# SBUF rooms of a hybrid decoder layer: the place of every take read from a table, in columns cut anew

## The chip, the cores and the metric

The kernel runs on one core of one Trainium2 chip, in one launch. The metric is the device time of one execution in microseconds. Before the change it is 1494.37 us, the median of three runs that lie between 1493.93 and 1495.05 us.

On the core, TensorE (PE in the profile; its weight loads are PEld) does the matrix products into PSUM. VectorE (DVE), ScalarE (ACT) and GpSimd (POOL) do the element-wise work. SyncE (SP) issues the DMAs; its queue is SPq in the rows.

## The reference, cut to what matters

One step of one decoder layer over 512 prompt tokens, 16 meta tokens and 32 sampled tokens (8 sequences of 4), 560 columns in all. The model is 1024 wide, the feed-forward 2816.

```python
h = x + 0.5 * rms_norm(swiglu(rms_norm(x, ffn1_pre_g), ffn1_w_gate, ffn1_w_up, ffn1_w_down), ffn1_post_g)
u = rms_norm(h, mix_pre_g)
proj = u @ w_in
q_a, k_a, v_a, gk_low, r_a, q_b, k_b, v_b, gate_a, gate_b = jnp.split(proj, offs, axis=-1)
...
o_a, s_new = gla_branch(q_a, k_a, v_a, g, s0.astype(f32), lead)
o_b = sb_attend(q_b, keys, vals, sb_bias, q_off).reshape(B, L, SB_W)
m = jax.nn.sigmoid(gate_a) * (o_a @ w_o_gla) + jax.nn.sigmoid(gate_b) * (o_b @ w_o_sb)
h = h + rms_norm(m @ w_out, mix_post_g)
y = h + 0.5 * rms_norm(swiglu(rms_norm(h, ffn2_pre_g), ffn2_w_gate, ffn2_w_up, ffn2_w_down), ffn2_post_g)
```

All values are float32. `gla_branch` is a gated linear recurrence in chunks of 64 tokens, four heads; `sb_attend` is stick-breaking attention, sixteen heads, over a paged cache for the sampled tokens.

## The kernel before, in words

**Products.** Activations lie with the feature on the partition and the 560 tokens along the row, in two halves of 280 columns. Each float32 factor is split in two fp32r parts, `hi` and `lo`, and each product is three matmuls: hi·hi, hi·lo, lo·hi (L686, L687, L689; L699, L700, L702; L1253 to L1255 and others). A weight block takes this road: SP loads it to a buffer `raw` (a pool of three; issued at L186 or L625), ACT casts it to `hi` (L665, L964), DVE subtracts to get `lo` (L153, the shared helper `tt`), and PE uses it. Many feed-forward tiles use a seven-product scheme on quarters of the blocks (`seven`, L1253 to L1255), the others the plain eight (`eight`).

**Stages.** FFN1, then the mixer (projections, the GLA heads, the stick-breaking heads, gates and output projections), then FFN2. Each feed-forward ends with its down projection (class `Down` and `k_steps`).

**What sets the order.** The program is written as one stream of steps. `step()` is called between groups of matmuls; `later(n, f)` puts a piece of element-wise work n steps ahead. For PE, DVE, ACT and POOL the order so written is kept (`manual_schedule`, L1462). The order of SP is not in that list: there the scheduler places each DMA where its buffer is ready, so the order in which SP issues loads and stores depends on when a buffer's last user is done.

**Rooms.** Everything that isn't in a fixed tile or a ring of the pools lives in an `Arena`: 150 units of 280 float32 columns, cut into columns: before, 20 long columns of 6 units and 15 short ones of 2. `take(width, dt)` hands out a run of free units in one column, a "room"; `give` returns it. A column holds one type (F32 or F32R) at a time. When an empty column changes its type it gets a new tile under the same tag, in the same bytes, and the first write to that tile waits for all that used the old one. A write to a room of a tile that goes on waits for whoever read or wrote those bytes last. So the place of a room decides for whom its first writer waits, and on SP also where a load stands. Before the change, `take` tries every free run and picks the one with the least key: it keeps four long columns in reserve, avoids runs at odd units, avoids rooms given less than `RECENT` = 14 steps ago, and among the rest takes the one that has been free longest.

**Names used below.** `h_again` (L1297 to L1299) loads the eight blocks of the FFN1 input `h` back from DRAM into rooms while the down projection of FFN1 runs. `fetch_early` (L635 to L638) loads a 512 KB weight block of the mixer's v projection to a room, ahead of its time. L1600 loads the 16 columns of `w_in` that give the low-rank gate, 64 bytes to a piece, into a room `wg16`; the DVE operation at L1602 multiplies them by `g_mix`. At L376 POOL clears a quarter of `t3`, a room of a GLA head, which `sample_keys` (L501 to L504) reads first. L469, L495 and L497 are POOL's causal masks of the GLA heads. `hidden` (L931) splits a finished feed-forward tile into rooms for `hi` and `lo`.

Of the kernel before, what the change touches and what calls it, by code (L numbers as in the profile page):

```python
# [9 lines left out]
F32 = mybir.dt.float32  # L10
F32R = mybir.dt.float32r
# [5 lines left out]
P = 128  # L17
# [5 lines left out]
NT = NP + NS + NM  # L23
# [22 lines left out]
MIXER += [("R", "p", 4), ("R", "p", 5), ("S", "b", 6), ("R", "p", 6), ("R", "p", 7)]  # L46
AHEAD = 150
LEAVE = 12
UNITS, LONGS = 150, 20


class Arena:

    UNIT = HW
    LONG, SHORT = 6, 2
    RECENT, RESERVE = 14, 4

    def __init__(self, pool, n, longs):
        self.pool, self.now, self.made = pool, 0, 0
        self.freed = [[-99] * self.LONG for _ in range(longs)]  # L60
        self.freed += [[-99] * self.SHORT for _ in range((n - longs * self.LONG) // self.SHORT)]
        self.tile = [None] * len(self.freed)
        self.held = {}

    def take(self, width, dt=F32, tight=False):
        k = -(-width // self.UNIT)
        best = None
        spare = sum(None not in f for f in self.freed if len(f) == self.LONG)
        for c, free in enumerate(self.freed):
            empty, long = None not in free, len(free) == self.LONG  # L70
            if not empty and self.tile[c].dtype != dt:
                continue
            for s in range(len(free) - k + 1):
                f = free[s : s + k]
                if None in f:
                    continue
                other = empty and self.tile[c] is not None and self.tile[c].dtype != dt
                since = max(free) if other else max(f)
                waste = k % 2 == 0 and s % 2
                alone = k == 1 and free[s ^ 1] is not None  # L80
                opens = empty and long and k <= self.SHORT
                key = (opens and spare <= self.RESERVE, waste, self.now - since < self.RECENT, opens, alone, since)
                if best is None or key < best[0]:
                    best = (key, c, s)
        assert best is not None, f"no room for {width}: {[sum(x is not None for x in f) for f in self.freed]}"
        _, c, s = best
        if None not in self.freed[c] and (self.tile[c] is None or self.tile[c].dtype != dt):
            self.made += 1
            self.tile[c] = self.pool.tile([P, len(self.freed[c]) * self.UNIT], dt, tag=f"room{c}", name=f"room{c}_{self.made}")
        self.freed[c][s : s + k] = [None] * k  # L90
        a = self.tile[c][:, s * self.UNIT : s * self.UNIT + width]
        self.held[id(a)] = (a, c, s, k)
        return a

    def halves(self, a):

        _, c, s, k = self.held.pop(id(a))
        r = a[:, :HW], a[:, HW:]
        for i, t in enumerate(r):
            self.held[id(t)] = (t, c, s + i, 1)  # L100
        return r

    def give(self, *aps):
        for a in aps:
            _, c, s, k = self.held.pop(id(a))
            self.now += 0.001
            self.freed[c][s : s + k] = [self.now] * k


class Parts:  # L110
# [11 lines left out]
def hybrid_step(  # L122
# [29 lines left out]
    def tt(out, a, b, op, eng=None):  # L152
        (eng or V).tensor_tensor(out=out, in0=a, in1=b, op=op)  # L153
# [128 lines left out]
    class Gates:  # L282
# [48 lines left out]
    class Head:  # L331
# [361 lines left out]
    def k_steps(acc, parts, k0, k1, kt, act, halves, nw=P, wid=(HW, HW)):  # L693
        hi, lo = parts
        for k in range(k0, k1):
            a = {h: act.get(k, h, wid[h]) for h in halves}
            wh, wl = hi[k - k0], lo[k - k0]
            for h in halves:
                T.matmul(acc[h][:nw, : wid[h]], wh, a[h][0], start=(k == 0), stop=False)  # L699
                T.matmul(acc[h][:nw, : wid[h]], wh, a[h][1], start=False, stop=False)  # L700
            for h in halves:
                T.matmul(acc[h][:nw, : wid[h]], wl, a[h][0], start=False, stop=(k == kt - 1))  # L702
            step()
# [19 lines left out]
    def later(n, f):  # L723
        todo.append([n, f])
# [314 lines left out]
    def early_tiles(u, rs, wid, nw, hid, pairs, wait, prepare, first=False):  # L1039
# [41 lines left out]
    def other_tiles(old, gain, rs, nw, wid, hid, pairs, plan, late, sums_at, begun):  # L1081
# [373 lines left out]
    for kind, what, n in MIXER:  # L1455
        w, c = {"r": (win, C_RA), "a": (win, C_GA), "b": (win, C_GB), "o": (w_o_gla[0], 0), "p": (w_o_sb[0], 0)}[what]
# [5 lines left out]
    with tc.manual_schedule(engines={E.PE, E.DVE, E.Activation, E.Pool}):  # L1462
# [72 lines left out]
        for j in range(2):  # L1535
            c = slice(P * j, P * j + P)
# [53 lines left out]
        hid = Parts()  # L1590
# [150 lines left out]
        for j in range(5):  # L1741
            n = P if j < 4 else NTL
# [89 lines left out]
    own_, other = (slice(0, 64), slice(64, P)), (slice(64, P), slice(0, 64))  # L1832
# [18 lines left out]
    class Pair:  # L1851
# [181 lines left out]
        at = property(lambda self: self.__dict__.setdefault("at_", {}))  # L2033
# [387 lines left out]
    with tc.manual_schedule(engines={E.PE, E.DVE, E.Activation, E.Pool}):  # L2421
# [5 lines left out]
        starts, n = {}, -24  # L2427
# [40 lines left out]
        for pr in range(9):  # L2468
            now = last = None
            at = {}  # L2470
# [67 lines left out]
            n = 0  # L2538
# [29 lines left out]
        n = 8 * len(PAGES)  # L2568
# [43 lines left out]
        n = 0  # L2612
# [42 lines left out]
        hid, pairs = Parts(), {}  # L2655
# [83 lines left out]
```

## Time and profile before

| | |
|---|---|
| time, median of three | 1494.37 us (1493.93 to 1495.05) |
| the profiled execution's own time | 1495.05 us |
| its span in the profile | 1493.4 us |
| mean granted clock of TensorE | 0.999 |
| instructions in the span | 29839 |
| HBM read / written | 155.06 MB / 24.97 MB |

The span runs from the first to the last instruction; 1.7 us of the execution's time lie around it. Rows of the profile give: line of the kernel, engine, operation, what is written and read (names without buffer numbers), shape, count, and then busy time or duration. An engine's idle time is put down to what ended it (`<-`). In a timeline, a row that stands for several instructions gives the stretch from the first's start to the last's end, and a bracket gives the idle time before it and its end.

### The profile page before, as it was taken

Reading aid. Unit: us, or ns where it says so; the run is one execution under the profiler, and the core shown is the slowest. Engines: PE = TensorE matmul, PEld = TensorE weight load, DVE = VectorE, ACT = ScalarE, POOL = GpSimd, SP = SyncE. Lnnn points to the kernel's source line nnn. Section 1 sums busy time; section 2 is a strip of 40 time slices with the busy share of each in tenths; the row PEclk is TensorE's granted clock in tenths of the full one; section 3 lists DMA queues with packets and bytes.
Section 4 is the critical chain, followed back from the end, with each engine's and each line's share of the span. In section 5 each row is a group of like instructions: output and inputs, shape, how many; then the busy total and the mean of one; then the engine's idle time right before and its main releaser. Section 6 shows DMA issues by size and latency. Waiting matters only on the chain.

```text
span 1493.4 us, 29839 instructions
## 1 busy us (share of the span) xinstructions
PE 1484.9 (99%) x11893; PEld 1434.2 (96%) x11893; DVE 1105.0 (74%) x1961; ACT 778.9 (52%) x1445; POOL 68.3 (5%) x146
## 2 busy tenths in 40 slices
PE   9999999999999999999999999999999999999998
PEld 8999999999999889999898999999999999999998
DVE  5888888855677866877887845777567898888544
ACT  7455454533555656556555543634565555455333
POOL 2000000000000011112111000000000000000000
PEclk9999999999999999999999999999999999999999
DMA  8133333224664584344456766434531333333262
GB/s 252 47 96 100 100 94 104 86 79 123 177 154 124 162 144 100 89 111 116 119 121 181 216 160 184 122 98 137 169 102 63 100 100 99 100 105 93 80 179 88
DMA packets 277229, 181.98 MB, mean 122 GB/s; under 512 B 10428, under 2 KB 255362, under 8 KB 277090
## 3 DMA queue, kind: packets, MB, share of 16 engines
q1 hardware_dynamic: 276786, 180.00, 44.5%
q8 instruction: 94, 1.54, 0.4%
q14 instruction: 45, 0.37, 0.1%
q0 software_dynamic: 288, 0.07, 0.0%
q10 hardware_dynamic: 16, 0.00, 0.0%
HBM read 155.06 MB, written 24.97 MB: 121 GB/s over the span
## 4 chain that ended last, share of the span: by engine, by line
PE 95%; DVE 3%; ACT 1%; issue 1%; DVEq 0%; ACTq 0%
PE acc L1253 8%; PE acc L1254 8%; PE acc L1255 8%; PE acc L686 7%; PE acc L687 7%; PE acc L689 7%; PE acc L699 6%; PE acc L702 6%; PE acc L700 6%; PE acc L1033 2%; PE acc L1034 2%; PE acc L1035 2%; PE acc L1196 1%; PE acc L1193 1%; DVE room L153 1%; PE acc L1194 1%
## 5 line engine op out<-in xcount | busy, mean ns | idle before, releaser
L153 DVE TENSOR_TENSOR lo<-raw,hi 128x1024 fp32r<-128x1024 f32 (+1 forms) x207 | 248.0, 1199 | 106.3 <-ACT hi L665 70.5
L153 DVE TENSOR_TENSOR room<-room,room 128x544 fp32r<-128x544 f32 (+16 forms) x424 | 263.3, 643 | 71.3 <-ACT room L766 16.6
L1253 PE MATMUL acc<-room,hi 128*128 128x280 f32 (+1 forms) x896 | 259.5, 290 | 0.0
L1254 PE MATMUL acc<-room,hi 128*128 128x280 f32 (+1 forms) x896 | 259.1, 289 | 0.0
L1255 PE MATMUL acc<-room,lo 128*128 128x280 f32 (+1 forms) x896 | 258.9, 289 | 0.0
L686 PE MATMUL acc<-room,hi 128*128 128x280 f32 x832 | 244.4, 310 | 0.2 <-DVE room L156 0.2
L687 PE MATMUL acc<-room,hi 128*128 128x280 f32 x832 | 225.2, 289 | 0.0
L964 ACT CAST hi<-raw 128x1024 fp32r<-128x1024 f32 x100 | 104.8, 1052 | 144.7 <-PE acc L1254 70.6
L689 PE MATMUL acc<-room,lo 128*128 128x280 f32 x832 | 172.9, 289 | 0.0
L1254 PEld LDWEIGHTS acc<-room,hi 128*128 128x128 f32 x896 | 168.6, 188 | 0.0
L1255 PEld LDWEIGHTS acc<-room,lo 128*128 128x128 f32 x896 | 168.6, 188 | 0.0
L1253 PEld LDWEIGHTS acc<-room,hi 128*128 128x128 f32 x896 | 168.6, 188 | 0.0
L686 PEld LDWEIGHTS acc<-room,hi 128*128 128x128 f32 x832 | 156.7, 188 | 12.0 <-issue 10.0
L687 PEld LDWEIGHTS acc<-room,hi 128*128 128x128 f32 x832 | 157.1, 189 | 2.8 <-issue 1.9
L665 ACT CAST hi<-raw 128x1024 fp32r<-128x1024 f32 (+1 forms) x107 | 108.2, 1012 | 73.8 <-issue 23.9
L689 PEld LDWEIGHTS acc<-room,lo 128*128 128x128 f32 x832 | 130.2, 188 | 0.0
L964 ACT CAST hi<-room 128x1024 fp32r<-128x1024 f32 x92 | 76.9, 836 | 87.8 <-PE acc L1254 59.4
L153 DVE TENSOR_TENSOR lo<-room,hi 128x1024 fp32r<-128x1024 f32 x92 | 87.8, 955 | 43.4 <-ACT hi L964 43.0
L699 PE MATMUL acc<-room,hi 128*128 128x280 f32 (+2 forms) x388 | 110.8, 295 | 0.0
L153 DVE TENSOR_TENSOR room<-room,acc 128x272 f32<-128x272 f32 (+1 forms) x180 | 76.3, 436 | 45.6 <-PE acc L1035 22.8
L700 PE MATMUL acc<-room,hi 128*128 128x280 f32 (+2 forms) x388 | 108.8, 290 | 0.0
L699 PE MATMUL acc<-room,room 128*128 128x280 f32 (+3 forms) x368 | 108.4, 295 | 0.0
(402 smaller groups left out, 3453.8 us busy)
## 6 DMA issues: line engine op xcount, KB each, us to landing
raw<-in_w_in_dram SPq DMA_DIRECT2D x43, 512.0 KB, 7.3
raw<-in_ffn_w_gate_dram SPq DMA_DIRECT2D x64, 256.0 KB, 3.0
raw<-in_ffn_w_up_dram SPq DMA_DIRECT2D x64, 256.0 KB, 3.4
raw<-in_ffn_w_down_dram SPq DMA_DIRECT2D x36, 448.0 KB, 4.0
raw<-in_w_in_dram SPq DMA_DIRECT2D x40, 256.0 KB, 5.3
out_dram<-room SPq DMA_DIRECT2D x36, 256.0 KB, 3.4
room<-in_cache_k_dram SPq DMA_DIRECT2D x32, 256.0 KB, 5.6
room<-in_cache_v_dram SPq DMA_DIRECT2D x32, 256.0 KB, 5.3
```

The lines of the kernel that those rows point to most:

```text
L153: (eng or V).tensor_tensor(out=out, in0=a, in1=b, op=op)
L665: S.copy(h_, src)
L686: T.matmul(acc[h][:, : wid[h]], hi[k], a[h][0], start=(k == order[0]), stop=False)
L687: T.matmul(acc[h][:, : wid[h]], hi[k], a[h][1], start=False, stop=False)
L689: T.matmul(acc[h][:, : wid[h]], lo[k], a[h][0], start=False, stop=(k == order[-1]))
L699: T.matmul(acc[h][:nw, : wid[h]], wh, a[h][0], start=(k == 0), stop=False)
L700: T.matmul(acc[h][:nw, : wid[h]], wh, a[h][1], start=False, stop=False)
L702: T.matmul(acc[h][:nw, : wid[h]], wl, a[h][0], start=False, stop=(k == kt - 1))
L964: S.copy(hi[:, :kt], src)
L1253: T.matmul(x[:, :QW], hi, act[k][0], start=(first and k == 0), stop=False, skip_group_check=True)
L1254: T.matmul(x[:, :QW], hi, act[k][1], start=False, stop=False, skip_group_check=True)
L1255: T.matmul(x[:, :QW], lo, act[k][0], start=False, stop=(k == 3), skip_group_check=True)
```

## The change

The search in `take` is replaced by a table, `PLACES`: one byte for each take in program order, the first unit of its room. The columns are cut anew: 14 long ones of 6 units and 33 short ones of 2, in the same 150 units. The arena keeps no more ages, only which units are free. `take` loses an argument that it didn't use, and `hidden` no longer passes it. Nothing else in the program's text differs; behind the table each line number is 13 higher.

```diff
-UNITS, LONGS = 150, 20
+UNITS, LONGS = 150, 14
+
+
+PLACES = bytes.fromhex("""
+0c06001e242a12181c888b747248687840524c445084465a6e8c7a42586064306a62566c827036764e5c906667227e547c9492305e868e3c3630
...
+""")
...
-    def take(self, width, dt=F32, tight=False):
-        k = -(-width // self.UNIT)
-        best = None
-        spare = sum(None not in f for f in self.freed if len(f) == self.LONG)
-        for c, free in enumerate(self.freed):
...
-                key = (opens and spare <= self.RESERVE, waste, self.now - since < self.RECENT, opens, alone, since)
...
+    def take(self, width, dt=F32):
+        k, s = -(-width // self.UNIT), next(self.places)
+        c, n = self.column(s)
+        assert all(self.free[s : s + k]) and s + k <= c + n, f"no room for {width} at {s}"
+        if c not in self.tile or self.tile[c].dtype != dt:
+            assert all(self.free[c : c + n]), f"two types at {c}"
             self.made += 1
-            self.tile[c] = self.pool.tile([P, len(self.freed[c]) * self.UNIT], dt, tag=f"room{c}", name=f"room{c}_{self.made}")
...
+            self.tile[c] = self.pool.tile([P, n * self.UNIT], dt, tag=f"room{c}", name=f"room{c}_{self.made}")
+        self.free[s : s + k] = [False] * k
+        a = self.tile[c][:, (s - c) * self.UNIT : (s - c) * self.UNIT + width]
+        self.held[id(a)] = (a, s, k)
         return a
...
-        hi, lo = hid.full[f] = take(NT, F32R, True), take(NT, F32R, True)
+        hi, lo = hid.full[f] = take(NT, F32R), take(NT, F32R)
```

On PE, ACT and DVE the instructions stand in the same order as before; the rooms that they name are others. On SP 279 of 657 positions hold another DMA than before, on POOL about a dozen positions another operation. Three places follow. In the rows, a room's first number counts the tiles that the arena has made and the second is the tile's own; `raw` buffers are numbered too.

SP, the end of FFN1's down projection: the loads of `h_again` (L1299, now L1312), of `fetch_early` (L638, now L651) and of the down weights (L186, now L199). Before:

```order
L1299 DMA room_55_4248<-h_dram 128x560
L1299 DMA room_54_4247<-h_dram 128x560 x2
L186 DMA raw_4144<-in_ffn_w_down_dram 128x8x128
L638 DMA room_57_4283<-in_w_in_dram 128x4x256
L186 DMA raw_4182<-in_ffn_w_down_dram 128x7x128
L186 DMA raw_4191<-in_ffn_w_down_dram 128x7x128
L186 DMA raw_4226<-in_ffn_w_down_dram 128x8x128
```

Now:

```order
L1312 DMA room_89_4282<-h_dram 128x560 x2
L651 DMA room_92_4318<-in_w_in_dram 128x4x256
L199 DMA raw_4179<-in_ffn_w_down_dram 128x8x128
L1312 DMA room_89_4282<-h_dram 128x560
L199 DMA raw_4217<-in_ffn_w_down_dram 128x7x128
L199 DMA raw_4226<-in_ffn_w_down_dram 128x7x128
```

The 512 KB load of `fetch_early` stood behind the down weights raw_4144; it now stands ahead of the same weights, which are raw_4179 in the changed program. One block of `h` that stood ahead of these weights now stands behind them.

SP, where FFN1's seven-product tiles end and its down projection begins: the load of the gate's 16 columns (L1600, now L1613) among the last gate and up weights (L625, now L638) and the first down weights. Before:

```order
L625 DMA raw_2722<-in_ffn_w_gate_dram 128x4x128
L1600 DMA room_40_991<-in_w_in_dram 128x8x16
L625 DMA raw_2777<-in_ffn_w_gate_dram 128x4x128
L625 DMA raw_2777<-in_ffn_w_up_dram 128x4x128
L625 DMA raw_2846<-in_ffn_w_up_dram 128x4x128
L625 DMA raw_2846<-in_ffn_w_gate_dram 128x4x128
L186 DMA raw_2901<-in_ffn_w_down_dram 128x8x128
```

Now:

```order
L638 DMA raw_2873<-in_ffn_w_up_dram 128x4x128
L638 DMA raw_2873<-in_ffn_w_gate_dram 128x4x128
L199 DMA raw_2928<-in_ffn_w_down_dram 128x8x128
L199 DMA raw_2996<-in_ffn_w_down_dram 128x8x128
L199 DMA raw_3050<-in_ffn_w_down_dram 128x7x128
L1613 DMA room_2_67<-in_w_in_dram 128x8x16
L199 DMA raw_3120<-in_ffn_w_down_dram 128x7x128
```

The small load goes from ahead of four gate and up weights to behind them and behind three down weights too.

POOL, the clearings of `t3` for the first two GLA heads and what lies between and behind them, with the semaphores that each waits for. Before:

```order
L376 MEMSET room_43_3190 32x384 [waits DMAHW4_49,DMAHW5_49,DVE_49,DMAHW7_49,PE_49,Pool_49]
L340 MEMSET dec_5423 128x20 [waits Pool_49]
L342 MEMSET st_1_5425 128x10
L376 MEMSET room_24_154 32x384 [waits DVE_49,PE_49,Pool_49]
L469 AFFINE_SELECT room_79_5434<-room_79_5434 128x512 [waits Activation_49,Pool_49]
```

Now:

```order
L389 MEMSET room_119_5298 32x384 [waits DMAHW1_49,DMAHW4_49,DVE_49,DMAHW5_49,PE_49,DMAHW6_49,Activation_49,Pool_49]
L353 MEMSET dec_5469 128x20 [waits Pool_49]
L355 MEMSET st_1_5471 128x10
L389 MEMSET room_129_5486 32x384 [waits PE_49,DVE_49,Activation_49,Pool_49]
L482 AFFINE_SELECT room_90_4283<-room_90_4283 128x512 [waits DMAHW0_49,Activation_49,Pool_49]
```

The same five operations stand in the same order, with other semaphores: both clearings of `t3` now also wait for ACT, and the first for other lanes of SP's DMAs.

More of the change, by code (lines that the diff above doesn't have):

```diff
@@ L48 @@
 LEAVE = 12
-UNITS, LONGS = 150, 20
+UNITS, LONGS = 150, 14
+PLACES = bytes.fromhex("""
+0c06001e242a12181c888b747248687840524c445084465a6e8c7a42586064306a62566c827036764e5c906667227e547c9492305e868e3c3630
+281666804a3e8a128a586c12302a36321e2c645c826a3418947c607e2454703a42903c3e0c065680664a92388676622e4e0c0054445e1e222016
+1214408c06684c487500568a7479845a7546520c548a6968106e8a508406565a5b7578680c00540d5a5b74246e06567a5b5a0c1a7900545a785b
+6e0a0d06560c8a725a180c00540d6f6e72260d06568a0c6f5a780d00547a6e6f0672080c5a097a6f0056020674036f6e0c8e0f005a280e296e04
@@ new lines @@
+0f060c7a757454287a000e746f6e065a090855540200068a62744a7a90107c4294367668346a92166e4e8c1412300c1e0e64066038027e785416
+868e8c3254182c562a4000862d7215413c1256245a73403c56402c3d8612733c2a57563c563c878640733d575606001e1856735b5a3e32907c52
+545086262d92108078345e72300e7e0c565a582e5c1c2c3c2a827a702874267b456660244c421131330d7d51643a38487a4e364a3e931453357f
+79860f555f916a45849468766c6972866f8e8c68466a1b42441a70683e18416e74402426676665646761602866240636384a1e6264404c583054
+5e5a34327e0402907c801092486064007a54820a3a08501a0b0c0e2e212062144e267863327e405a7a5c3818644c8212522c001c544a0c04328a
@@ new lines @@
+080e0d0a363a7e2866143462637f245e162e067a1e5c0c1864100e404a2002789222045a0d3e362866627a7c3a380926240807603c4e6564807e
+100c7a06404c3e110b0a9066085c622c2a7c0f5600286424888a1918835458821062607e535c7c805e88241650120e04273022651e8a567e5a5b
+58546078808288625e5c7e92537c5682556160785c5a8a7e80889262585e647c5482568a4a555e5a6078648892585c7e627c538058825b5a2078
+5456605e7c7e88642c62801c5c8233922a5a62022c8a53327e7c5e58605c882e3464821478628054568a1c2c92181a20885a623a4e484a936400
+545682607814025c3c347e62805e582e2c20322a88367838627c92484a4b3a3460585c5a147e20825e3c5400626456807c48537e780220364e3c
@@ new lines @@
+14545682924b4a324838005a645c3a3602343c5a125e541658626014925024565e82522058620e644a305c4b4e3a066628400a90602620225662
+04480a3258001e58243c0102521034364a569138603a4e00500c2624906206664050286160020a10014004383a48603c00324e520c3634605632
+0a484a3462900c660636000a4862643a30324a040e40663c025c0690105d04383632313011084c7a003a48664a3e641004363831624d7a085d00
+405c320206663c64485c304c4a3a386662902636524e8254282053555e1624405664543c60585955007a1e2256543e6459625863006250825832
+4e5235067a9034915654626390910006906234327a580a0b5756060c00746884945a54566c768c92882a42722c44206a805c481a6e605e406730
@@ new lines @@
+3a38344b862e26661b15183646243c1532287078161514157c8e8a7e4c4b12682c4e6474901a662e8626184a48507a586244821b403038341b60
+6f6e3b3a151b425c722a1b5e60141b49695559655756226a155a5b547583451c8876914f7b8d4c4a1e846c7680128e7c5270948a182e3c863e24
+164866787e30600c0604624038885e6a36345c320c00547a4e12142a3a1e2022820656908c5b0c586e5a6f7472056e5000545604570e5a0d7274
+0656580c590a040e00580f0d0c5a68100656110c0d0e0a1800585a5b060c101a06561b5a5b0e180c00580d5b5a061a080c560900025a1c010658
+2425000e0c26005a272406425425060e29280026564300244229284458460626424300280e450024444243080629280203260046447e646c8482
@@ L52 @@
+3c32685e8e306a5c345a02047660801e3e42187c54088a78100a02865c94563676880858120624880a00022a7658590658100e110f000c0d5859
+0c100f080659090e585812060c2a761e581a2059763a2218633690301c345a702e
+""")
 class Arena:
@@ L55 @@
     LONG, SHORT = 6, 2
-    RECENT, RESERVE = 14, 4
     def __init__(self, pool, n, longs):
[L59 to L63, printed above, removed]
-    def take(self, width, dt=F32, tight=False):
-        k = -(-width // self.UNIT)
-        best = None
-        spare = sum(None not in f for f in self.freed if len(f) == self.LONG)
-        for c, free in enumerate(self.freed):
[L70 to L81, printed above, removed]
-                key = (opens and spare <= self.RESERVE, waste, self.now - since < self.RECENT, opens, alone, since)
[L83 to L87, printed above, removed]
@@ new lines, in __init__, with column @@
+        self.pool, self.now, self.made, self.longs = pool, 0, 0, longs
+        self.free, self.held, self.tile = [True] * n, {}, {}
+        self.places = iter(PLACES)
+    def column(self, s):
+        n = self.LONG * self.longs
+        return (s - s % self.LONG, self.LONG) if s < n else (s - (s - n) % self.SHORT, self.SHORT)
+    def take(self, width, dt=F32):
[4 more added lines that the diff above has]
+            assert all(self.free[c : c + n]), f"two types at {c}"
@@ L93, in take @@
+        self.held[id(a)] = (a, s, k)
         return a
     def halves(self, a):
-        _, c, s, k = self.held.pop(id(a))
+        _, s, k = self.held.pop(id(a))
         r = a[:, :HW], a[:, HW:]
         for i, t in enumerate(r):
-            self.held[id(t)] = (t, c, s + i, 1)
+            self.held[id(t)] = (t, s + i, 1)
         return r
@@ L104, in give @@
         for a in aps:
-            _, c, s, k = self.held.pop(id(a))
-            self.now += 0.001
-            self.freed[c][s : s + k] = [self.now] * k
+            _, s, k = self.held.pop(id(a))
+            self.free[s : s + k] = [True] * k
 class Parts:
```

3 lines of the change are left out of this document (removed).

## The prediction

> **What bounds the kernel now.** I read the page's head and chain first, then the list of TensorE's waits, then the groups of its matmuls.
>
> ```profile
> span 1493.4 us, 29839 instructions
> PE 1484.9 (99%) x11893; PEld 1434.2 (96%) x11893; DVE 1105.0 (74%) x1961; ACT 778.9 (52%) x1445; POOL 68.3 (5%) x146
> PE 95%; DVE 3%; ACT 1%; issue 1%; DVEq 0%; ACTq 0%
> ```
>
> TensorE is busy for 1484.9 of 1493.4 us and carries 95% of the chain that ended last. All its idle time is 8.5 us, the start and the end of the program among it. The view of waits names what ended the part that lies inside (waiting line, releaser; total, times, longest):
>
> ```profile
> PE acc L1480 <- DVE own L257: 1.1, 1, 1.1
> PE acc L830 <- DVE room L153: 0.4, 1, 0.4
> PE ps L2233 <- DVE room L2203: 0.4, 1, 0.4
> PE ps L1561 <- DVE room L1560: 0.4, 1, 0.4
> PE acc L686 <- DVE room L156: 0.2, 1, 0.2
> PE ps L860 <- DVE room L153: 0.2, 1, 0.2
> ```
>
> Six waits, 2.7 us. The first is on `own`, a fixed tile that no table moves. The other five are 1.6 us in all. None is on a DMA, and none is long. So the change has two ways to matter: it can take away some of 1.6 us, or it can make TensorE wait where it doesn't wait now.
>
> How far the other engines run ahead decides the second. The views of waits and of DMA issues show:
>
> ```profile
> ACT hi L964 <- PE acc L1254: 130.0, 115, 2.2
> DVE lo L153 <- ACT hi L964: 77.4, 86, 4.2
> ACT hi L665 <- DMA raw<-in_ffn_w_down_dram: 10.4, 6, 4.4
> raw<-in_ffn_w_down_dram SPq DMA_DIRECT2D x36, 448.0 KB, 4.0
> raw<-in_ffn_w_down_dram SPq DMA_DIRECT2D x10, 512.0 KB, 4.2
> ```
>
> In the seven-product tiles ACT waits for PE 115 times, 130 us in all: the casts run as far ahead as their buffers let them, and a load that comes a little late is absorbed. The place to look at is the down projection, where ACT waits for a DMA, up to 4.4 us at once. A weight block takes 4.0 to 4.2 us from issue to landing in the median there.
>
> **The change part by part.** No engine gets an instruction more, and on PE, ACT and DVE the order is the old one; the work itself costs 0. What the change can cost or save is waiting. The sum has four terms.
>
> *Term 1, the load of `fetch_early` ahead of a down weight.* SP issues, ACT's casts, DVE's `lo` and the matmuls that need them, from the timeline:
>
> ```profile
> 363.26 1.29 SPq L1299 DMA_DIRECT2D room<-h_dram  x3
> 365.91 0.38 SPq L186 DMA_DIRECT2D raw<-in_ffn_w_down_dram  x1
> 366.34 0.58 SPq L638 DMA_DIRECT2D room<-in_w_in_dram  x1
> 370.27 1.05 ACT L665 CAST hi<-raw 128x1024 fp32r<-128x1024 f32 x1 [1.22 <-DMA raw<-in_ffn_w_down_dram]
> 375.71 0.94 ACT L665 CAST hi<-raw 128x896 fp32r<-128x896 f32 x1 [4.39 <-DMA raw<-in_ffn_w_down_dram]
> 377.29 0.94 ACT L665 CAST hi<-raw 128x896 fp32r<-128x896 f32 x1 [0.64 <-DMA raw<-in_ffn_w_down_dram]
> 371.35 1.23 DVE L153 TENSOR_TENSOR lo<-raw,hi 128x1024 fp32r<-128x1024 f32 x1 [1.11 <-ACT hi L665]
> 374.43 0.29 PE L699 MATMUL acc<-room,hi 128*128 128x280 f32 x1
> 374.68 0.29 PE L702 MATMUL acc<-room,lo 128*128 128x280 f32 x1
> ```
>
> The block issued at 365.91 reaches the cast at 370.27, 4.36 us later: hardly more than the median of 4.2. Two more blocks follow, and between them and it lies the load of `fetch_early`. From 370.27 to 375.71 pass 5.44 us, with that load and one 448 KB block in the queue; from there to 377.29 pass 1.58 us, for one 448 KB block alone. So the load holds the queue for 5.44 − 1.58 = 3.86 us. Now it stands ahead of the weight block, so that the block can land up to 3.86 us later. Some of that is given back: with one `h` load fewer ahead, `fetch_early` can go out at the end of the second of three, about 363.26 + 2/3 × 1.29 = 364.1, some 1.7 us before the block's 365.91. I estimate 2.2 (3.86 − 1.7) to 3.86 us of delay, and take 2.7, since the block's room in its ring keeps its own issue where it was and the `h` load no longer ahead takes part of the time in between.
>
> The slack is the distance from `lo` to its reader: 371.35 + 1.23 = 372.58 against 374.68, which is 2.1 us. (`hi` ends at 370.27 + 1.05 = 371.32 and is read at 374.43: 3.1 us, more than 2.7.) TensorE then waits 2.7 − 2.1 = 0.6 us; between the bounds 0.1 and 1.8. The next block, cast at 375.71, has no slack at all, but the load that stood ahead of it still stands ahead of it: 0.
>
> By the Trainium skill, "DMA: Bandwidth & Descriptors", section "Queues, rings and completion order", descriptors of a ring are consumed in ring order, while completion is not first in, first out for each issuing engine: a later load can be complete before an earlier one. Taken at its word the block needn't wait for the whole load ahead, and this term would go from 0.6 us towards 0. The casts above follow the order of issue, so this trace rather shows queueing, but no row of it decides the case.
>
> *Term 2, the 64 KB load of L1600, later.* The timeline and the load's own view:
>
> ```profile
> 235.35 0.37 SPq L1600 DMA_DIRECT2D room<-in_w_in_dram  x1
> DMA to landing us min/median/max: 6.4/6.4/6.4
> 258.46 0.37 SPq L186 DMA_DIRECT2D raw<-in_ffn_w_down_dram  x1
> 264.67 0.37 SPq L186 DMA_DIRECT2D raw<-in_ffn_w_down_dram  x1
> 265.87 0.28 DVE L153 TENSOR_TENSOR room<-room,gains 128x128 f32<-128x128 f32 x1
> 274.02 1.09 DVE L153 TENSOR_TENSOR lo<-raw,hi 128x896 fp32r<-128x896 f32 x1 [1.13 <-ACT hi L665]
> ```
>
> It moves behind the third down weight (258.46), so from 235.35 to about 258.9, and lands at 258.9 + 6.4 = 265.3; its reader on DVE starts at 265.87. That is 0.5 us to spare; if it queues, DVE loses up to about 1 us, which the idle 1.13 us before its `lo` at 274.02 gives back. The next weight on SP isn't issued before 264.67, so nothing queues up behind it. I put 0, between 0 and 1 us on DVE, and 0 on TensorE. The gate and up weights that stood behind it move forward: no one waits for them.
>
> *Term 3, POOL's clearing of `t3` behind other waits.* POOL's and DVE's timeline:
>
> ```profile
> 445.44 0.41 POOL L376 MEMSET room<- 32x384 f32 x1 [48.89 <-DMA raw<-in_w_in_dram]
> 445.92 0.12 POOL L340 MEMSET dec<- 128x20 f32 x1
> 458.04 0.41 POOL L376 MEMSET room<- 32x384 f32 x1 [11.96 <-issue]
> 479.87 1.21 POOL L469 TENSOR_SCALAR_AFFINE_SELECT room<-room 128x512 f32<-128x512 f32 x1 [21.42 <-ACT room L468]
> 484.43 0.75 DVE L153 TENSOR_TENSOR room<-room,own 128x256 fp32r<-128x256 f32 x2
> ```
>
> Behind it on POOL stand the small clearings, a second `t3` at 458.04 and the mask L469, which waits for ACT until 479.87. The first reader of a `t3` is `sample_keys` on DVE at 484.43. So the first clearing can be 34 us late (445.44 to 479.87) before anything is late. If its new wait ended later than that, it would hold the mask too; the rows don't exclude it, but 34 us is longer than any wait of an engine other than POOL here. 0 at both ends.
>
> *Term 4, waits removed.* At most 1.6 us from the five rows above. Those are waits for a result (DVE's `room` that PE reads), which no place takes away, as far as the rows tell; I take 0, and keep −1.6 as the bound.
>
> The sum: +0.6 + 0 + 0 + 0 = +0.6 us, between −1.6 and +1.8 for these terms. On the profiled execution (1495.05 us, span 1493.4) that is 1495.7 and a span of 1494.0; on the median of 1494.37, from which this execution lies 0.7 us, it is **1495.0 us**. A measurement of this kernel (three runs within 1.1 us) tells about 0.2%, 3 us, from no change, so this is "the same".
>
> **The rivals.**
>
> *Reordered loads push weights past their slack at several places (slower).* 279 places of SP's order differ, and I worked out two. Each load that comes ahead of a weight block costs at most its time in the queue less the slack: 3.86 − 2.1 = 1.8 us at term 1's upper bound. Three more such places make 4 × 1.8 = 7.2 us: 1501.6 us. It decides as soon as two places reach their bound (3.6 us). For it: the down projection's casts do wait for DMAs (10.4 us over 6 times). Against it: none of these six waits shows in TensorE's list, and the seven-product tiles have ACT waiting for PE. Near term 1 TensorE isn't idle in any stretch, with the queue filled beyond its share:
>
> ```profile
> 363.00:369.00 6.00, 6.00 (x48) 6.00 (x47) 4.99 (x10) 4.95 (x10) 0.00 (x0) 1.00 0.73 221
> 375.00:381.00 6.00, 6.00 (x47) 5.88 (x46) 2.54 (x3) 2.57 (x4) 0.00 (x0) 1.00 1.06 277
> ```
>
> (stretch; busy us of PE, PEld, DVE, ACT, POOL with counts; granted clock; DMA share; GB/s.)
>
> *The waits go (faster).* All 1.6 us: 1492.8 us. That isn't yet faster by 0.2%. For more, TensorE's pace itself would have to depend on where its operands lie, since every operand moves.
>
> *Pace by place (either side).* The matmul groups, mean ns of one behind the busy time:
>
> ```profile
> L1253 PE MATMUL acc<-room,hi 128*128 128x280 f32 (+1 forms) x896 | 259.5, 290 | 0.0
> L1255 PE MATMUL acc<-room,lo 128*128 128x280 f32 (+1 forms) x896 | 258.9, 289 | 0.0
> ```
>
> These 896 and 896 matmuls read rooms and rings at other places and agree within 1 ns. If the moves changed the pace by 0.5%, that would be 0.005 × 1484.9 = 7.4 us: 1487.0 or 1501.8 us. Nothing in the profile speaks for it.
>
> *The change doesn't do what it says.* If only places changed and every wait ended where it ended, the time would be 1494.4 us. It can't be told from the forecast; the SP rows above say that it does a little more.
>
> **How the numbers follow.** Forecast together with "no effect" and "the waits go" 0.70; reordered loads at several places 0.18, most of it above 1497.4; pace by place 0.10, half on each side; 0.02 for something faster that I don't see. Slower by over 0.2% is then 0.16 + 0.05 = 0.21, faster 0.05 + 0.02 = 0.07, the same 0.72. The low end: 1494.37 − 1.6 = 1492.8, less 0.4 for the spread below the median (1493.93), 1492.4. The high end: two places at their bound and a third, 3 × 1.8 = 5.4 us, 1499.8. The forecast's own range is 1492.8 to 1496.2.
>
> **What would show it.** Term 1: a wait of TensorE at the line of L702 (now L715) near 374.7 us, 0.1 to 1.8 us, and the cast of that block 2 to 4 us later. Term 2: L1613 issued near 259 us and no wait on TensorE near 266. Term 3: the first `t3` cleared after 445.4 and before 480 us, the mask at 480 in place. Term 4: the five waits as before. The forecast is wrong if the view of TensorE's waits sums to more than 5 us, above all with DMA or `lo` as releasers in the down projections or the head stage, or if the mean of the 896-fold groups moves by over 1 ns.

## The result, and the profile after

| | before | changed |
|---|---|---|
| time, median (13 runs each) | 1494.72 us | 1499.0 us |
| lowest to highest | 1493.93 to 1495.77 | 1497.36 to 1500.4 |
| profiled execution: time, span | 1495.05, 1493.4 | 1497.98, 1496.0 |

The ratio is 1.0027, with a 95% interval of 1.002 to 1.0034: slower by about 4 us. The forecast was 1495.0 and "the same", with 1492.8 to 1496.2 for its own terms. The time lies outside of that and inside the whole range (1492.4 to 1499.8), whose upper part was there for the rivals. The runs of the changed kernel also spread over 3.0 us, those of before over 1.8.

The page's head and its chain of the changed kernel:

```profile
span 1496.0 us, 29848 instructions
PE 1486.5 (99%) x11893; PEld 1435.6 (96%) x11893; DVE 1105.5 (74%) x1961; ACT 778.1 (52%) x1445; POOL 69.1 (5%) x146
PE 95%; DVE 2%; DMA 1%; SPq 1%; ACT 1%; issue 0%; DVEq 0%; ACTq 0%
```

A DMA and SP's queue have come into the chain, with 1% each, and TensorE is busy for 1.6 us more (1486.5 against 1484.9) with the same 11893 matmuls. (The nine instructions that the span has more are none of the counted ones on PE, DVE, ACT and POOL.) The wait and the busy time are two different things, and the views below take them apart. First TensorE's waits in the changed kernel (waiting line, releaser; total, times, longest):

```profile
PE acc L1493 <- DVE own L270: 1.1, 1, 1.1
PE acc L712 <- ACT hi L678: 0.9, 1, 0.9
PE acc L715 <- DVE lo L166: 0.7, 1, 0.7
PE ps L1574 <- DVE room L1573: 0.5, 2, 0.4
PE acc L843 <- DVE room L166: 0.4, 1, 0.4
PE ps L2246 <- DVE room L2216: 0.4, 1, 0.4
PE ps L1551 <- DVE room L169: 0.2, 1, 0.2
PE ps L873 <- DVE room L166: 0.2, 1, 0.2
PE acc L699 <- DVE room L169: 0.2, 1, 0.2
```

The waits at L712 and L715 are new. Both are on one weight block; the timeline shows SP's issues ahead of it and ACT's cast of it (the view of DMA issues behind it gives L651's load, its last column the us from issue to landing):

```profile
363.85 0.82 SPq L1312 DMA_DIRECT2D room<-h_dram  x2
364.77 0.38 SPq L651 DMA_DIRECT2D room<-in_w_in_dram  x1
366.53 0.38 SPq L199 DMA_DIRECT2D raw<-in_ffn_w_down_dram  x1
...
374.94 1.04 ACT L678 CAST hi<-raw 128x1024 fp32r<-128x1024 f32 x1 [5.22 <-DMA raw<-in_ffn_w_down_dram]
```

The view of DMA issues of the same kernel:

```profile
room<-in_w_in_dram SPq DMA_DIRECT2D x1, 512.0 KB, 8.4
```

TensorE waits for `hi` and then for `lo`, 1.6 us together. The block was issued at 366.53 and cast at 374.94, 8.41 us later, against 4.36 before. The load of `fetch_early` (L651) stands in front of it, takes 8.4 us itself and lands at 373.2.

Second, the stretches of the seven-product matmuls: in the timeline of TensorE the first and the last of FFN1 and of FFN2. Before:

```profile
94.02 0.29 PE L1253 MATMUL acc<-room,hi 128*128 128x280 f32 x1
266.72 0.29 PE L1255 MATMUL acc<-room,lo 128*128 128x280 f32 x1
1182.10 0.29 PE L1253 MATMUL acc<-room,hi 128*128 128x272 f32 x1
1349.78 0.29 PE L1255 MATMUL acc<-room,lo 128*128 128x272 f32 x1
```

The changed kernel:

```profile
93.56 0.29 PE L1266 MATMUL acc<-room,hi 128*128 128x280 f32 x1
267.41 0.29 PE L1268 MATMUL acc<-room,lo 128*128 128x280 f32 x1
1184.70 0.28 PE L1266 MATMUL acc<-room,hi 128*128 128x272 f32 x1
1353.00 0.28 PE L1268 MATMUL acc<-room,lo 128*128 128x272 f32 x1
```

Each stretch holds 1344 matmuls and no wait in either kernel. In FFN1 it takes 172.70 us before and 173.85 us now, in FFN2 167.68 and 168.30: 1.15 and 0.62 us more. From one kernel to the other the single intervals between starts differ by 2.4 to 2.9 ns on the mean, either way; 0.66 ns to a matmul is what is left of it. Between the two stretches, from 266.72 to 1182.10 and from 267.41 to 1184.70, lie 1.91 us more, most of which is the wait. At the start 0.46 us are gained, and behind the last stretch 0.6 (143.6 us to the span's end before, 143.0 now): −0.46 + 1.15 + 1.91 + 0.62 − 0.6 = 2.6 us, which is the difference of the spans. The −0.6 at the end is not the change's: in b_shift below, which has before's layout and order, 142.8 us follow the last stretch too.

So two theories went to the chip. **Q**: the load ahead of the weights makes the wait near 374 us. **P**: TensorE's pace depends on where its operands lie. In these texts "the changed kernel" has a median of 1499.0 us.

### The profile page after: what moved, and what is told of

Its sections match the earlier page's. It is cut to its first block, busy times and chain, and to the rows that moved or that the text cites. A ratio compares the mean times of both kernels' runs of the same rounds, so it can differ in the third digit from the quotient of the medians.

```text
span 1496.0 us, 29848 instructions
## 1 busy us (share of the span) xinstructions
PE 1486.5 (99%) x11893; PEld 1435.6 (96%) x11893; DVE 1105.5 (74%) x1961; ACT 778.1 (52%) x1445; POOL 69.1 (5%) x146
## 4 chain that ended last, share of the span: by engine, by line
PE 95%; DVE 2%; DMA 1%; SPq 1%; ACT 1%; issue 0%; DVEq 0%; ACTq 0%
PE acc L1266 8%; PE acc L1268 8%; PE acc L1267 8%; PE acc L699 7%; PE acc L700 7%; PE acc L702 7%; PE acc L712 6%; PE acc L715 6%; PE acc L713 6%; PE acc L1046 2%; PE acc L1048 2%; PE acc L1047 2%; PE acc L1209 2%; PE acc L1206 2%; PE acc L1207 2%; PE ps L2041 1%
## 5 line engine op out<-in xcount | busy, mean ns | idle before, releaser
L166 DVE TENSOR_TENSOR room<-room,room 128x272 f32<-128x272 f32 (+14 forms) x453 | 281.5, 644 | 71.5 <-ACT room L779 17.8
L712 PE MATMUL acc<-room,hi 128*128 128x280 f32 (+2 forms) x388 | 110.9, 295 | 0.9 <-ACT hi L678 0.9
L715 PE MATMUL acc<-room,room 128*128 128x280 f32 (+3 forms) x366 | 106.2, 290 | 0.2
```

## The experiments

All kernels compute the whole layer. "Before" is measured anew with each group; its medians are 1494.83 (a_late, b_early, b_rev, a_rev), 1494.98 (b_perm, b_shift, a_later, a_late_rev), 1494.74 (b_others_ops, b_ops_others) and 1494.71 us (a_again, a_later_rev). Ratios are to the before of the same group.

**a_late: the load handed to SP four steps later.** In the changed kernel:

```diff
             self.early[r0, c0] = room = take(8 * P)
-            nc.sync.dma_start(room.rearrange("p (k n) -> p k n", n=2 * P),
-                              win[r0 : r0 + 4 * P, c0 : c0 + 2 * P].rearrange("(k p) n -> p k n", p=P))
+            later(4, lambda: nc.sync.dma_start(room.rearrange("p (k n) -> p k n", n=2 * P),
+                              win[r0 : r0 + 4 * P, c0 : c0 + 2 * P].rearrange("(k p) n -> p k n", p=P)))
```

> The changed kernel with the load of fetch_early handed to SP four steps later; its room and all other places are the table's. SP's order then differs from the changed kernel's in four positions: the load stands behind the down weights again. Theory Q (the load ahead of the weights costs TensorE its wait near 374 us): the 1.6 us of waits at L712 and L715 are gone, and the time falls by 1.6 to 2.2 us, from 1499.0 to about 1497. If that wait were the whole cost of the change, 1494.7. Rival P (TensorE's pace depends on where operands lie): about 1497, with the rest of the loss in matmuls that take longer without a wait. If the load has nothing to do with it: 1499.0.

Measured: 1496.63 us (1495.91 to 1498.71), ratio 1.0014 (1.0004 to 1.0023), 2.4 us less than the changed kernel. ACT's casts in its timeline:

```profile
371.29 1.05 ACT L678 CAST hi<-raw 128x1024 fp32r<-128x1024 f32 x1 [1.64 <-DMA raw<-in_ffn_w_down_dram]
376.83 0.94 ACT L678 CAST hi<-raw 128x896 fp32r<-128x896 f32 x1 [4.48 <-DMA raw<-in_ffn_w_down_dram]
```

TensorE's waits in the same kernel:

```profile
PE acc L715 <- DVE lo L166: 0.5, 1, 0.5
```

The block is cast 3.65 us earlier than in the changed kernel and the wait on it is gone. What is left is 0.5 us on the next block, the one that had no slack: the load lands ahead of that one. The order of issue here is that of before, where the same block came without a wait, cast at 375.71; why it comes 1.1 us later now, when the issues are 0.55 us late (366.89 against 366.34 for the load), isn't shown. Q holds for this part; that the time stays 1.8 us above before says that it isn't the whole.

**b_early: the other way round, the load ahead in the kernel before.** In the kernels whose names begin with b, before's places are written down as a table, with before's columns (`UNITS, LONGS = 150, 20`). Here two long columns are exchanged from the step of `h_again` on (58 takes move). One line of the table, with before's places and as exchanged:

```diff
...
-1a527c8688008a181e200c1a1423243e12283c488a17271e1817271a1b1e121327213c181217213d3c1821191a3642000c12211721488a8b706e
+1a527c8688008a181e200c1a1423243e12283c488a17271e1817271a1b1e121327213c181217213d3c1821191a360c004212211721488a8b706e
...
```

> The kernel before, its places written down as a table, with two long columns exchanged from the step at which h is loaded again, so that the load of fetch_early comes ahead of the down weights; SP's order differs from before in four positions. Q: a wait of TensorE near 374 us of 1.6 to 2.2 us and a time of about 1496.5 to 1497. P alone: 1494.7 within 0.5, since few places move. If the load is harmless: 1494.7 and no wait.

Measured: 1496.99 us (1496.59 to 1499.56), ratio 1.0017 (1.0008 to 1.0026). Its timeline of SP and ACT:

```profile
363.27 0.37 SPq L651 DMA_DIRECT2D room<-in_w_in_dram  x1
...
365.93 0.38 SPq L199 DMA_DIRECT2D raw<-in_ffn_w_down_dram  x1
...
374.19 1.05 ACT L678 CAST hi<-raw 128x1024 fp32r<-128x1024 f32 x1 [5.13 <-DMA raw<-in_ffn_w_down_dram]
```

TensorE's two new waits in it:

```profile
PE acc L715 <- DVE lo L166: 0.7, 1, 0.7
PE acc L712 <- ACT hi L678: 0.7, 1, 0.7
```

The load went out 2.7 us ahead of the block this time (363.27 and 365.93), and the block still was cast 8.26 us after its issue. The same two waits come up in the kernel before, 1.4 us together, and it is 2.2 us slower; another 0.73 us lies in FFN2's seven-product matmuls (168.41 us against 167.68; more of that below). Q is shown from both sides.

**b_rev and a_rev: only the addresses of the rooms.** Ahead of the first take a tile is made in each column, last column first, so that the columns lie in reverse order in SBUF; the order of every engine's instructions stays as it was:

```diff
         self.places = iter(PLACES)
+        for c in [148, 146, 144, ..., 12, 6, 0]:
+            pool.tile([P, self.column(c)[1] * self.UNIT], F32, tag=f"room{c}", name=f"first{c}")
```

> The kernel before with its columns laid out in reverse order in SBUF: every instruction, wait and place in the order is that of before, only the addresses of the rooms are others. P: the time moves by 1 us or more either way, with no wait of TensorE that before hasn't, and the mean interval of the matmuls in the seven-product tiles changes by 0.3 ns or more. Q alone: 1494.7 within 0.6 us.

> The changed kernel with its columns laid out in reverse order in SBUF: only addresses differ from the changed kernel. The wait near 374 us stays in every theory. P: the time moves by 1 us or more from 1499.0. Q alone: 1499.0 within 0.8 us.

Measured: b_rev 1495.86 us (1494.96 to 1496.57), ratio 1.0007 (0.9998 to 1.0016); a_rev 1497.31 us (1496.86 to 1499.15), ratio to before 1.0019 (1.001 to 1.0028). In a_rev the wait stays (0.8 us at the line of L712, 0.7 at that of L715) and 1.7 us go. Its seven-product stretches take 173.09 and 168.41 us, 0.76 less and 0.11 more than the changed kernel's, so 0.65 of the 1.7 us lie in them. b_rev is 1.0 us off before at the medians, but its interval takes in 1. Its stretches take 172.54 and 168.51 us (−0.15 and +0.83 from unrounded starts), 0.25 ns to a matmul, less than the 0.3 expected; and against what was expected its list of waits is longer than before's, by 0.7 us (0.9 instead of 0.4 at the line of L1561, 0.2 at that of L1538, which has none before). P is likely after these two, and not yet shown.

**b_perm: columns in an order drawn at random**, with the same edit as b_rev and another list.

> The kernel before with its columns laid out in an order drawn at random; every order and wait as before. P: a time between 1493 and 1497, off from 1494.8 by 0.5 us or more, the difference made of many matmuls by a few ns each and no wait. If addresses do nothing: 1494.8 within 0.4.

Measured: 1496.59 us (1495.29 to 1497.04), ratio 1.0009 (1.0 to 1.0018); the stretches take 173.32 and 168.74 us, together 1.7 us more than before. TensorE's list of waits is that of before but for 0.2 us at the line of L1538.

**b_shift: everything 32 bytes higher.**

```diff
+    cp.tile([P, 8], F32, name="pad")
     arena = Arena(cp, UNITS, LONGS)
```

> The kernel before with 32 bytes put ahead of the arena: every room and every ring of weight parts lies 32 bytes higher, with all distances among them and every order as before. P in the form that the distances of operands, or the parts of the address above 64 bytes, set the pace: 1494.8 within 0.5 us, and the matmuls of the seven-product tiles take what they take before. P in the form that the place within 64 bytes sets it: at least 1 us off, either way.

Measured: 1494.28 us (1493.6 to 1494.72), ratio 0.9994 (0.9985 to 1.0003), 0.5 us below the 1494.8 expected. TensorE's timeline at the ends of the two stretches:

```profile
93.98 0.29 PE L1267 MATMUL acc<-room,hi 128*128 128x280 f32 x1
266.68 0.29 PE L1269 MATMUL acc<-room,lo 128*128 128x280 f32 x1
1182.24 0.29 PE L1267 MATMUL acc<-room,hi 128*128 128x272 f32 x1
1349.92 0.29 PE L1269 MATMUL acc<-room,lo 128*128 128x272 f32 x1
```

These are 172.70 and 167.68 us, before's own numbers. This says two things: the stretches repeat to 0.01 us from execution to execution, so that differences of tenths are readable; and a shift of all operands by half of 64 bytes, which leaves the distances among them, doesn't change the pace.

**b_others_ops and b_ops_others: whose addresses.** In before's table, rooms move inside their own columns. In the first kernel, those that the seven-product matmuls of FFN1 don't read, and in FFN2 those that they do; in the second the other way round. The first line of the table, with before's places and with those of b_others_ops:

```diff
-00060c12181e242a161c22787a7c7e80828486888a8c8e90929430323436383c282e3a424446484e50525423404c5a565860625c6466686a6c72
+00060c141a20262a12181f787a7c7e80828486888a8c8e90929430323436383e242e3a4244464a4e5052541e3d485e565860625a6466686a6e74
...
```

> The kernel before with rooms moved inside their columns and nothing in an engine's order changed. In FFN1 the rooms that move are those that the seven-product matmuls don't read (DVE's and ACT's temporaries and results); in FFN2 those that they do read (624 of 1344 operands). P1 (the pace hangs on TensorE's own operands): the 1344 seven-product matmuls of FFN1 take what they take before, to within 0.05 us in all, and those of FFN2 differ by 0.2 us or more. P2 (DVE and ACT get in TensorE's way in some places of SBUF): FFN1's differ by 0.2 us or more, FFN2's less.

> The same the other way round: in FFN1 the rooms that the seven-product matmuls read move (800 of 1344 operands), in FFN2 those that they don't read. P1: the seven-product matmuls of FFN1 differ from before by 0.2 us or more in all, those of FFN2 by less than 0.05 us. P2: the other way round. The time: 1494 to 1497 us in both.

Measured: 1496.05 us (1495.23 to 1497.11), ratio 1.0008 (0.9998 to 1.0018), and 1495.93 us (1494.89 to 1497.05), ratio 1.0009 (0.9999 to 1.0018). The times decide nothing; the stretches do. b_others_ops:

```profile
94.60 0.29 PE L1266 MATMUL acc<-room,hi 128*128 128x280 f32 x1
267.29 0.29 PE L1268 MATMUL acc<-room,lo 128*128 128x280 f32 x1
1182.72 0.29 PE L1266 MATMUL acc<-room,hi 128*128 128x272 f32 x1
1351.14 0.29 PE L1268 MATMUL acc<-room,lo 128*128 128x272 f32 x1
```

b_ops_others:

```profile
94.01 0.29 PE L1266 MATMUL acc<-room,hi 128*128 128x280 f32 x1
267.69 0.29 PE L1268 MATMUL acc<-room,lo 128*128 128x280 f32 x1
1182.92 0.29 PE L1266 MATMUL acc<-room,hi 128*128 128x272 f32 x1
1350.61 0.29 PE L1268 MATMUL acc<-room,lo 128*128 128x272 f32 x1
```

Against 172.70 and 167.68 us: the first kernel has 172.69 and 168.42, the second 173.68 and 167.69. Where TensorE's operands stay, the stretch stays within 0.01 us, whatever DVE and ACT write elsewhere; where they move, it is 0.74 or 0.98 us longer. P1 is shown, P2 is refuted. That b_early's FFN2 stretch is 0.73 us longer (168.41) fits too: 176 of its 1344 operands lie in the two exchanged columns. But the time isn't lost at the moved operands themselves: 0.59 of these 0.73 us fall on matmuls that stand more than two places from any that reads a moved room. So P1 says whose addresses matter, not how.

**a_later, a_late_rev and a_later_rev: do the two costs add up?** a_later is a_late with `later(16, ...)`, a_late_rev is a_late with the reversed columns, a_later_rev has both.

> The changed kernel with the load of fetch_early sixteen steps later, behind four down weights instead of one. Q: the wait of 0.5 us that was left at L715 with four steps goes too, and the time is 1496.0, 0.6 below that with four steps; the load is still in time for its own use. If the wait left comes from the blocks of h instead: 1496.6 and the wait stays.

> The changed kernel with both edits: the load of fetch_early four steps later, and the columns in reverse order. If the two costs are apart and add up: 1499.0 less 2.4 (the first edit alone gave 1496.6) less 1.7 (the second alone 1497.3), 1494.9 us within 0.6. If both edits mend the same thing: 1496.6 to 1497.3.

> The changed kernel with the load of fetch_early sixteen steps later and the columns in reverse order. If the wait and the pace add up: 1495.3 (four steps later, reversed) less 0.5 (what the twelve further steps gave alone) = 1494.8 us, the same as before within 0.5 us; no wait at L712 or L715 near 374 us, and 173.09 and 168.41 us for the two stretches of seven-product matmuls.

Measured: a_later 1496.15 us (1495.72 to 1497.05), ratio 1.001 (1.0 to 1.0019); a_late_rev 1495.32 us (1494.59 to 1496.59), ratio 1.0001 (0.9992 to 1.001); a_later_rev 1494.55 us (1494.12 to 1495.12), ratio 0.9998 (0.9989 to 1.0007). In a_later the block with no slack is cast at 374.90 instead of 376.83, and the wait left by four steps is gone:

```profile
371.91 1.05 ACT L678 CAST hi<-raw 128x1024 fp32r<-128x1024 f32 x1 [1.94 <-DMA raw<-in_ffn_w_down_dram]
374.90 0.95 ACT L678 CAST hi<-raw 128x896 fp32r<-128x896 f32 x1 [1.95 <-DMA raw<-in_ffn_w_down_dram]
```

TensorE's waits in a_later_rev are before's six, with the same tenths; no wait is left at L712 or L715, and its stretches take the 173.09 and 168.41 us of a_rev.

Each time expected from the sum is met within 0.5 us. With both edits the changed kernel's table runs as fast as before, 1494.55 against 1494.71 us, and its runs lie within 1.0 us of each other. The times add up, but the traces don't bear out that the stretches are what the reversal mends: it takes 1.3 to 1.7 us off the medians (a_late to a_late_rev, the changed kernel to a_rev) and 0.65 us off the stretches, and in a_later_rev these are still 1.12 us longer than before's (341.50 against 340.38 us together). What makes up for it lies elsewhere; 0.84 us of it between the two stretches (914.54 us against 915.38). No version was found that is measurably faster than before: its layout has the least sum of the two stretches of the eight measured (340.38 us; the others have 341.05 to 342.15).

**a_again: the changed kernel once more.**

> The changed kernel as it is, profiled a second time. The seven-product matmuls of both feed-forwards take what they took in the first profile, to within 0.05 us (173.85 and 168.30 us from the first to the last); the wait near 374 us stands on DMAs and may differ, 1.5 to 3.5 us. The time: 1498 to 1499.5 us.

Measured: 1500.03 us (1497.23 to 1500.79), ratio 1.0032 (1.0021 to 1.0043): above what was expected. The stretches are 173.85 and 168.30 us, as in the first profile, and the waits at L712 and L715 are 0.5 and 0.7 us. The profiled execution itself took 1497.69 us; five of its eight runs took over 1499.5. So part of the loss, some 2 us in such executions, is in none of the two traces. It lies inside the program: the span is 1495.8 us in the profiled execution and 1497.9 to 1498.9 in those five. From a_again to a_later the median falls by 3.9 us, more than the 1.2 to 1.6 us of waits in the traces, and no run of a_later or a_later_rev stands out like this. But with the load ahead and other addresses such executions are rare: one of eleven in a_rev (1499.15, median 1497.31) and one in b_early (1499.56, median 1496.99). As far as these runs tell, it takes the place of the load and the changed kernel's addresses together. What the loads do in the longer executions wasn't seen.

## Why the prediction came out as it did

**What bounds the kernel.** Right: TensorE, with no wait on a DMA before.

**Term 1, the load ahead of a down weight.** The mechanism, the place, the line and the direction were right; the size was off. The delay of the block was taken as 2.7 us, at most 3.86; it was 4.05 (8.41 − 4.36). With that number the working gives what came: 372.58 + 4.05 − 374.68 = 1.95 us, where 0.6 was forecast and the two waits show 1.6. The step that failed is the balance of 3.86 us held and 1.7 us "given back" because the load goes out earlier. In b_early it goes out even 2.7 us ahead of the block, and the block still came 3.9 us late (8.26 − 4.36). `hi`, to which 3.1 us of slack were given, became late too.

Why so little of it comes back, the view of stretches of the changed kernel shows (columns as in the prediction; the last two are DMA share and GB/s):

```profile
368.00:370.00 2.00, 2.00 (x18) 2.00 (x17) 2.00 (x5) 1.72 (x4) 0.00 (x0) 1.00 0.27 97
372.00:374.00 2.00, 2.00 (x18) 2.00 (x17) 0.00 (x0) 0.00 (x0) 0.00 (x0) 1.00 1.05 317
```

The load of `fetch_early` is slow in itself. In the first row mostly its pieces move, in the second mostly those of down weights. Before, it has 370 to 372 us nearly to itself, at 106 GB/s and a share of 0.29. Its packets (1 KB each; those of the weights have 512 bytes) end between 366.75 and 372.80 us in the changed kernel and between 364.34 and 370.51 in b_early: 6.1 and 6.2 us, where 3.86 had been taken from the gaps between casts. Less the head starts of 1.8 and 2.7 us that leaves 4.3 and 3.5 us, an estimate from these rows, against 4.05 and 3.9 measured. The block is cast after the last of those packets, at 374.94 and 374.19. What holds the load to a third of the rate isn't shown. Before's view of DMA issues had a possible sign of it: the other large blocks of `w_in` take 7.3 us to land in the median, where down weights of the same size take 4.2. Whether the cause is the same isn't shown.

```profile
raw<-in_w_in_dram SPq DMA_DIRECT2D x43, 512.0 KB, 7.3
```

The rule of the Trainium skill that the prediction weighed ("DMA: Bandwidth & Descriptors", section "Queues, rings and completion order": a later load can be complete before an earlier one) would have brought this term towards 0. It says what can happen, and the trace shows that here it didn't: the load ahead landed at 373.2 us (364.77 + 8.4) and the block was cast at 374.94.

**Term 2, L1613.** Right: issued at 259.72, no wait of TensorE near 266. DVE's product with `g_mix` starts 0.67 us later than before, which is what the whole trace is late by there (0.69 at the stretch's end): nothing lost.

```profile
259.72 0.37 SPq L1613 DMA_DIRECT2D room<-in_w_in_dram  x1
266.54 0.29 DVE L166 TENSOR_TENSOR room<-room,gains 128x128 f32<-128x128 f32 x1
```

**Term 3, POOL's clearing.** Right: the first clearing is 10.3 us later (455.76), and the mask behind it 2.53 us, as late as TensorE is by then:

```profile
455.76 0.41 POOL L389 MEMSET room<- 32x384 f32 x1 [50.20 <-ACT room L1711]
482.40 1.23 POOL L482 TENSOR_SCALAR_AFFINE_SELECT room<-room 128x512 f32<-128x512 f32 x1 [21.87 <-DMA raw<-in_w_in_dram]
```

**Term 4, the waits that were there.** Right: all six still stand in the changed kernel's list, five with the same tenths and that of L1561 (now L1574) with 0.1 more.

**The rival "pace by place"** was given 0.10, and its slower half was what happened together with term 1. It was put aside for a reason that doesn't bear: that the groups of 896 matmuls agree within 1 ns on the mean. Each group's mean runs over dozens of places, so that all groups agree whether or not a place matters; and 0.66 ns, which is below what was looked at, is 1.8 us over 2688 matmuls. Nor are the 290 ns of those rows the pace: the matmuls overlap and start 128.5 ns apart (172.70 us for 1344). The test that would have told it is a comparison of the same matmul in two layouts, which before's trace alone doesn't hold.

**The rival "several places"** didn't happen in the two traces of the changed kernel: apart from the two waits of term 1, the first has only 0.2 us at L1551 and 0.1 at L1574 that before hasn't, and a_again 0.3 at L1574 and two of 0.2; none is on a DMA. The 0.2 at L1551 also stands in b_shift, so it needs no other layout. For the longer executions the rival stays open.

So of the 4.3 us, 2.4 (a_late) to 2.9 (a_later) go with the load: 1.2 to 1.6 as waits in the traces, the rest in longer executions that no trace holds. What is left in a_later, 1.2 us over before, has no new wait but the 0.2 at L1551 and is of the size of the 1.77 us that the two stretches take longer. The reversal takes 1.7 us off the changed kernel and 1.6 off a_later, 0.65 of it in the stretches; the rest isn't located.

**The range.** That 1499.0 us lies inside the range is luck. Its upper end was three places at 1.8 us each, and there was one place. What filled it is term 1 taken 1.0 us too small, the pace, and the longer executions, which the prediction doesn't have. Its signs were too coarse for both: the waits sum to 4.6 us where over 5 was to be the sign, and the means of the 896-fold groups move from 290, 289 and 289 ns to 290.

## What to carry to other kernels

Where a queue's order is left to a scheduler that goes by readiness, a change of buffers is a change of the order of loads: compare the order of issue, look for a large load that has moved ahead of a weight with little slack, and charge it at its own rate, read from a stretch in which it moves (here about 100 GB/s, against some 300 for the weights), rather than from the gaps between later casts. A load that nobody needs soon should be handed to the queue later by hand, behind the weights that are needed now; here that took 2.4 to 2.9 us off the median. When TensorE is busy 99% of the time, compare the length of stretches without waits between two layouts before a tenth of a per cent is put down to anything else.

## What the runs showed of the hardware

TensorE's pace depends on where its moving operands lie. Over 1344 matmuls without a wait, eight layouts of the rooms gave 172.54 to 173.85 us in FFN1 and 167.68 to 168.74 us in FFN2, up to 0.8%; each layout repeats to 0.01 us between executions (173.85 in four profiles with the changed kernel's layout). Moving everything by 32 bytes changes nothing (172.70 and 167.68 us in b_shift), and where the rooms lie that these matmuls don't read changes nothing (172.69 in b_others_ops, 167.69 in b_ops_others). Which relation of addresses costs the nanoseconds stays open.

The loads of one queue moved at very different rates: about 100 GB/s (97 and 106) at a DMA share of 0.27 to 0.29 while the block of `w_in` moves, 317 GB/s at 1.05 while down weights do. The weight block that was issued 1.8 us (changed kernel) or 2.7 us (b_early) behind the slow one was cast 8.41 and 8.26 us after its issue, against 4.36 with that load behind it.
